# Attention beside a gated recurrence: four engines in written order, one decay copy per level, a third pair of sums on VectorE

## The chip, the cores and the metric

The kernel runs on one core of one Trainium2 chip. The metric is device time in microseconds (us). An engine takes its instructions in the order of its queue; PE is TensorE (PEld its weight loads), DVE is VectorE, ACT is ScalarE, POOL is GpSimd, SP is the queue that issues the DMAs. [...]

## What is computed

One layer of a diffusion backbone over 2048 latent and 256 context tokens, all in fp32: a normalised and modulated input, one projection, then two groups of heads side by side (softmax attention with 8 query and 2 key heads, and a gated linear recurrence with 4 heads that runs in both directions), their joint output projection, and a SwiGLU block. The change is in the two groups of heads:

```python
s = jnp.einsum('bqkgd,bnkd->bkgqn', q, keys).astype(jnp.float32) * scale
p = jax.nn.softmax(s, axis=-1)
return jnp.einsum('bkgqn,bnkd->bqkgd', p.astype(vals.dtype), vals)
...
S_new = jnp.exp(b_last)[..., None] * S + jnp.einsum('bhsk,bhsv->bhkv', kc * jnp.exp(b_last[:, :, None, :] - b), vc)
...
o = rmsnorm(o_f + flip(o_b), gain).reshape(Bn, T, HG_WIDTH)
return (o * jax.nn.silu(g.astype(jnp.float32))).astype(g.dtype)
```

## The kernel before

The program goes through five stages: modulation, projection, attention beside recurrence, output projection, SwiGLU. The change is in the third, the `with` block from line 610 on.

**Attention.** 32 items (16 blocks of 128 queries for each of the 2 key heads), each of 18 steps, one step for each tile of 128 keys. The global step is `x`, `n` the item and `k` the step in it. A step (`Item.scores`, L992) multiplies keys and queries in two matmuls (L1000, L1001: high and low part) into one of three PSUM banks `s`, and ACT takes the exponential into half of a tile `p` (L1004): a pair of steps fills 1024 columns. Beside it a step does one chunk of the next item's maxima (`Item.chunk`, L961): a matmul into one of two banks `mx` (L969, L975) and a reduction on DVE (L971, L977); `Item.maxima` (L983) transposes the result `pn` through a bank of pool `ps_h` and writes it into the next item's queries. Every six steps is an *event* (steps 8, 14 and 20, the last being step 2 of the next item): `Item.products` (L1013) multiplies the last six exponentials by the values (L1020), and sums them over the keys with 32 columns of ones (L1028). The sums take two groups of matmuls for a batch: one over `ps`, the sum of the first two pairs that POOL made (`Item.add`, L1008), one over the third pair `p`. `drain` (L1032) empties the bank, takes the reciprocal of the sums, and `finish` (L1038) scales.

**Recurrence.** A `Unit` (L628) is 512 tokens of a head (unit 0 the 256 of the context). It goes through seven *levels*, in each of which blocks of 1, 2, ... 64 tokens are joined. Two lanes of units run, one level of each per *round*; two rounds fall in an item, at the events of steps 8 and 14. In a round PE makes the scores `pa` from the tiles `Q` and `M` (L684), DVE copies them under a mask into `A` (L694), POOL multiplies `M`, `C` and both halves of `Q` by decays (L703, L706, L715, L717), ACT copies the other halves of `M` and `C` into new tiles (L709, L710), and DVE makes the next level's decays `T` (L721). `prepare` (L649), `diagonal` (L667), `keys` (L726), `forward` (L738), `chain` (L779) and `output` (L786) are steps around it; `output` makes `po` on PE, squares it on ACT, sums it on DVE (L798), takes the root on POOL (L799), and `store` scales it on DVE (L807) and multiplies by the gate on POOL.

**Order.** PE and DVE keep the order in which the code is written (`manual_schedule`, L1080 and L1159; SP too in the first item); the instructions of ACT and POOL are placed by the scheduler from its own estimate of times. At which step a piece of the recurrence is written is set by the table `STEPS` (L1077) and by `Recurrence.plan` (L822). Behind the last item (L1101 on) stand the loads and casts of the output projection's weights (`wos`, `woh` L1121, `wol` L1122) and its first tokens (`mix_token`, L1128).

Of the kernel before, what the change touches and what calls it, by code (L numbers as in the profile page):

```python
# [16 lines left out]
P = 128  # L17
# [51 lines left out]
def block_kernel(ctx: ExitStack, tc: tile.TileContext, a: dict, out: bass.AP, dbg=None):  # L69
# [540 lines left out]
    with ExitStack() as st:  # L610
# [16 lines left out]
        mask = hc.tile([P, 7, P], I32, name="mask")  # L627
        class Unit:  # L628
# [3 lines left out]
            def __init__(self, h, u):  # L632
                self.h, self.u = h, u
                self.n = 256 if u == 0 else 512
                self.nch = self.n // P
                self.t0 = 0 if u == 0 else 256 + (u - 1) * 512
                self.lv = 0
                self.kt = [None, None]

# [9 lines left out]
            def prepare(self):  # L649
                h, u, n, F = self.h, self.u, self.n, self.F  # L650
                M = up.tile([P, 512], F32, tag="M", name=f"M{h}{u}_0", bufs=4)
                C = up.tile([P, 512], F32, tag="C", name=f"C{h}{u}_0", bufs=4)
                pair = "p (j s) -> p j s"
                nc.scalar.activation(M[:, :n].rearrange(pair, s=2), strided(F[:], 0, [[4, n // 2], [3, 2]]),
                                     AF.Identity, scale=-1.0, bias=1.0)
                nc.scalar.activation(C[:, :n].rearrange(pair, s=2), strided(F[:], 1, [[4, n // 2], [1, 2]]),
                                     AF.Identity, scale=-1.0, bias=1.0)
                self.M, self.C, self.T = M, C, F
# [8 lines left out]
            def diagonal(self):  # L667
# [4 lines left out]
                nc.scalar.activation(self.A, pa, AF.Copy)  # L672

# [14 lines left out]
            def level(self, pa=None):  # L688

                h, u, n, lv, M, C, Tt = self.h, self.u, self.n, self.lv, self.M, self.C, self.T  # L690
                hs = 1 << lv
                nb = n // hs
                if u:
                    nc.vector.copy_predicated(  # L694
# [3 lines left out]
                M2 = up.tile([P, 512], F32, tag="M", name=f"M{h}{u}_{lv + 1}", bufs=4)  # L698
                C2 = up.tile([P, 512], F32, tag="C", name=f"C{h}{u}_{lv + 1}", bufs=4)
                g4 = nb // 4  # L700
                odim = [[4 * hs, g4], [3 * hs, 2], [1, hs]]
                if nb >= 4:
                    nc.gpsimd.tensor_tensor(strided(M2[:], 0, odim), strided(M[:], 0, odim),  # L703
                                            strided(Tt[:], 2, [[8, g4], [3, 2], [0, hs]]), op=ALU.mult)
                    idim = [[4 * hs, g4], [hs, 2], [1, hs]]
                    nc.gpsimd.tensor_tensor(strided(C2[:], hs, idim), strided(M[:], hs, idim),  # L706
                                            strided(Tt[:], 1, [[8, g4], [5, 2], [0, hs]]), op=ALU.mult)
                    cdim = [[4 * hs, g4], [1, 2 * hs]]
                    nc.scalar.activation(strided(M2[:], hs, cdim), strided(C[:], hs, cdim), AF.Copy)  # L709
                    nc.scalar.activation(strided(C2[:], 0, odim), strided(C[:], 0, odim), AF.Copy)  # L710
                if u:
                    Q4 = self.Q.rearrange("p d (j s h) -> p d j s h", s=2, h=hs)
                    T3 = Tt[:, :nb, :].rearrange("p (j s) d -> p j s d", s=2)
                    sh = [P, nb // 2, hs]
                    nc.gpsimd.tensor_tensor(Q4[:, 1, :, 1, :], Q4[:, 1, :, 1, :],  # L715
                                            T3[:, :, 0, 0][:, :, None].to_broadcast(sh), op=ALU.mult)
                    nc.gpsimd.tensor_tensor(Q4[:, 0, :, 0, :], Q4[:, 0, :, 0, :],  # L717
                                            T3[:, :, 1, 1][:, :, None].to_broadcast(sh), op=ALU.mult)
                T2 = up.tile([P, nb // 2, 2], F32, tag=f"T{lv}", name=f"T{h}{u}_{lv}",
                             bufs=8 if lv == 6 else 2)  # L720
                nc.vector.tensor_reduce(T2, Tt[:, :nb, :].rearrange("p (j s) d -> p j d s", s=2),  # L721
# [90 lines left out]
        class Recurrence:  # L812
# [40 lines left out]
            def context(self, h):  # L853
# [3 lines left out]
                for _ in range(4):  # L857
                    yield
# [934 lines left out]
```

## Time and profile before

| | |
|---|---|
| median of 3 runs | 3236.01 us (3235.59 to 3236.52) |
| the profiled execution | 3230.49 us, its span 3228.7 us |
| granted PE clock over the span | 0.993 |
| the stretch of attention and recurrence | 727 to 1740 us of the span |
| busy in it: PE, DVE, ACT, POOL | 986, 605, 520, 684 us |
| the 192 groups of sums (L1028) | 2 x 1536 matmul records, 61.9 and 59.5 us busy |
| POOL's 96 additions of pairs (L1011) | 229.9 us, 2395 ns each |
| reductions of the maxima (L971) | 496, 685 ns each |

How to read it: a row of groups gives line, engine, operation, output and inputs, shapes, count, then busy us and the mean ns of one, then the idle time ahead of them with what ended it. A row of the timeline gives start, length, line and operation, and in brackets the idle time ahead of it. A row of waits says who waited for whom, the total, how often, the longest. fp32 matmuls stand twice in the records, once for each of two passes. Matmuls are pipelined, so their busy times overlap.

### The profile page before, as it was taken

What the parts mean: (1) busy time and instruction counts of PE and PEld (TensorE: products, weight loads), DVE (VectorE), ACT (ScalarE), POOL (GpSimd) and SP (SyncE); (2) the same over time, 40 slices, a digit from 0 to 9 for tenths busy, and PEclk for the clock granted to TensorE, in tenths of its full rate; (3) what the DMA queues carried; (4) which work ended last, traced back from release to release, by engine and by line L of the source; (5) the groups of instructions that cost most, each with busy time, mean ns of one, the idle gap of its engine ahead of it and who ended that gap; (6) DMA issues with size and microseconds to landing.
All of it is one profiled execution on the core that took longest, in us unless ns stands there. A gap on an engine that the chain in (4) does not pass through costs nothing. (4 is left out here: it accounts for less than half of the span.)

```text
span 3228.7 us, 55815 instructions
## 1 busy us (share of the span) xinstructions
PE 3145.3 (97%) x21212; PEld 2559.5 (79%) x21212; DVE 1755.1 (54%) x3070; ACT 1326.6 (41%) x2563; POOL 1575.1 (49%) x1403
## 2 busy tenths in 40 slices
PE   8999999999999999999999999999999999999998
PEld 5998987896777777777777887888877778888886
DVE  6344555416666665665653656445458753333566
ACT  4422222215554555554543225333335443333344
POOL 4322222206767767776634226777600168776222
PEclk9999999999999999999999999999999999999999
DMA  7243544324111211211006435555575533332665
GB/s 246 92 137 125 153 145 146 119 93 121 31 36 46 67 34 49 59 37 48 28 21 201 134 115 183 196 179 189 173 291 195 193 111 115 108 104 98 243 195 185
DMA packets 368999, 406.86 MB, mean 126 GB/s; under 512 B 31285, under 2 KB 260889, under 8 KB 368346
## 3 DMA queue, kind: packets, MB, share of 16 engines
q1 hardware_dynamic: 368730, 403.30, 38.9%
q8 instruction: 166, 2.72, 0.4%
q14 instruction: 103, 0.84, 0.1%
HBM read 273.34 MB, written 129.78 MB: 125 GB/s over the span
## 5 line engine op out<-in xcount | busy, mean ns | idle before, releaser
L971 DVE TENSOR_REDUCE mn<-mx 128x1 f32<-128x512 f32 x496 | 333.9, 685 | 209.7 <-PE mx L969 204.6
L1004 ACT ACTIVATE p<-s 128x512 f32<-128x512 f32 x576 | 338.5, 598 | 167.3 <-PE s L1001 147.5
L1011 POOL TENSOR_TENSOR ps<-p,p 128x1024 f32<-128x1024 f32 x96 | 229.9, 2395 | 162.3 <-ACT p L1004 162.3
L1020 PE MATMUL av<-p,VS 128*64 128x256 f32 x2304 | 268.7, 382 | 0.0
L1000 PE MATMUL s<-qa,K 128*128 128x512 f32 x576 | 253.4, 440 | 10.8 <-ACT p L1004 10.8
L1001 PE MATMUL s<-qb,KB 128*128 128x512 f32 x576 | 227.4, 395 | 0.0
L1020 PEld LDWEIGHTS av<-p,VS 128*64 128x64 f32 x2304 | 158.9, 138 | 82.5 <-issue 13.9
L969 PE MATMUL mx<-K,qa 128*128 128x512 f32 x496 | 200.9, 406 | 2.7 <-DVE mn L971 2.4
L1621 DVE TENSOR_TENSOR dl<-dl,x 128x512 fp32r<-128x512 f32 x154 | 113.7, 761 | 70.8 <-ACT x L1614 69.9
L1000 PEld LDWEIGHTS s<-qa,K 128*128 128x128 f32 x576 | 109.0, 189 | 47.9 <-issue 19.8
L1614 ACT ACTIVATE x<-dl 128x512 fp32r<-128x512 f32 x154 | 96.2, 631 | 106.1 <-DMA dl<-s_hid0A 41.1
L1614 ACT ACTIVATE dh<-dl 128x512 fp32r<-128x512 f32 x154 | 89.0, 623 | 93.7 <-PE pd1A L1682 48.3
L345 PE MATMUL f<-hTh,wh 128*128 128x512 f32 (+1 forms) x320 | 120.8, 377 | 6.9 <-ACT ft L374 6.9
L969 PEld LDWEIGHTS mx<-K,qa 128*128 128x128 f32 x496 | 93.4, 188 | 41.4 <-DVE mn L971 17.8
L1621 DVE TENSOR_TENSOR dl<-dl,dh 128x512 fp32r<-128x512 f32 x154 | 102.0, 688 | 43.1 <-ACT dh L1614 42.0
L122 POOL TENSOR_TENSOR rs_xf<-ms_xf,mhalf 128x1 f32<-128x1 f32 x16 | 12.7, 803 | 227.6 <-DVE ms_xf L120 227.6
L345 PE MATMUL f<-hTh,wl 128*128 128x512 f32 (+1 forms) x320 | 118.5, 370 | 0.0
L345 PE MATMUL f<-hTl,wh 128*128 128x512 f32 (+1 forms) x320 | 118.4, 370 | 0.0
L1001 PEld LDWEIGHTS s<-qb,KB 128*128 128x128 f32 x576 | 109.6, 190 | 10.9
L1445 PE MATMUL pA<-x,A22h 128*128 128x512 f32 x352 | 108.9, 391 | 4.5 <-DVE r L1518 4.5
L1445 PE MATMUL pA<-x,A11h 128*128 128x512 f32 x352 | 110.7, 395 | 2.4 <-ACT A11h L1414 2.4
L1445 PE MATMUL pC<-x,A12h 128*128 128x512 f32 x352 | 112.0, 391 | 0.0
(373 smaller groups left out, 9337.0 us busy)
## 6 DMA issues: line engine op xcount, KB each, us to landing
w<-in_w_gu_dram SPq DMA_DIRECT2D x88, 512.0 KB
wm<-in_w_mod_dram SPq DMA_DIRECT2D x24, 1024.0 KB
dl<-s_wT SPq DMA_DIRECT2D x88, 256.0 KB
dl<-s_wB SPq DMA_DIRECT2D x66, 256.0 KB
wq<-in_w_down_dram SPq DMA_DIRECT2D x44, 256.0 KB
s_wT<-wq SPq DMA_DIRECT2D x44, 256.0 KB
dl<-s_hid1S SPq DMA_DIRECT2D x44, 256.0 KB
dl<-s_hid0S SPq DMA_DIRECT2D x44, 256.0 KB
```

The lines of the kernel that those rows point to most:

```text
L122: nc.gpsimd.tensor_tensor(rs, ms, mhalf[:, :width], op=ALU.pow)
L345: nc.tensor.matmul(pm[:, :n], w[wi][:, k, c0:c0 + P], hT[b][hi][:, k, :], start=(k == 0 and i == 0), stop=(k == KT - 1 and i == 2))
L969: nc.tensor.matmul(s, self.qa[:, h * P:(h + 1) * P], K[:, k * 512:(k + 1) * 512], start=True, stop=True)
L971: nc.vector.tensor_reduce(self.mn[:, h, k:k + 1], s, axis=AX.X, op=ALU.min)
L1000: nc.tensor.matmul(s, KS[self.g][:, ks], self.qa, start=True, stop=False)
L1001: nc.tensor.matmul(s, KB[k // BATCH][:, k % BATCH * P:(k % BATCH + 1) * P], self.qb, start=False, stop=True)
L1004: nc.scalar.activation(self.pairs[p][:, o:o + 512], s, AF.Exp, scale=-1.0)
L1011: nc.gpsimd.tensor_tensor(t, self.pairs[p - 1], self.pairs[p], op=ALU.add)
L1020: nc.tensor.matmul(self.av[i * 64:(i + 1) * 64, :256], VS[:, k, self.g * 64:(self.g + 1) * 64], self.pairs[k // 2][:, o:o + 256], start=(k ...
L1445: nc.tensor.matmul(acc, w[wi][:, k, :], x[xi][k], start=(start and k == 0 and i == 0), stop=(stop and k == KH - 1 and i == 2), skip_group_ ...
L1614: nc.scalar.activation(hi, f32v(lo), AF.Copy)
L1621: nc.vector.tensor_tensor(lo, f32v(lo), f32v(hi), op=ALU.subtract)
```

## The change

- **Sums.** A batch is now described by `SUMS = ".PE.PE.PE"`: of each three pairs POOL adds the second to the first (P), and DVE adds the third at the event (E), just ahead of the products. One group of sums is left per batch.
- **Order.** ACT and POOL are written in order too. All pieces of the recurrence stand in lists of global steps; `later` puts an instruction some steps behind.
- **Level.** `C` is changed in place instead of being copied (L710 goes), the two multiplications of `Q` become one instruction of 512 columns, and `T` is made ahead (`extend`): the first at a step of its own, the next ones at the event without a round.
- **Readout.** ACT squares and sums by chunk of 128 (`accum_out`) and scales by chunk, three steps later; DVE's two operations go.
- **Reciprocal.** `drain` copies the sums too, and `invert` takes the reciprocal from SBUF at step 8 instead of step 3; `finish` goes from step 5 to 10.
- **Banks and tiles.** `pn` takes a bank of the `mx` pool. The values are in three tiles of 64 columns, loaded anew for the second key head. Minima chunks start eight instead of six steps ahead.

The core of it (a few of the moved steps' tables and the context's small functions are left out):

```diff
+        LACT, LPOOL, TE = 0, [0, 0, 0], 2
+        KC, STT = 0, 1
...
+        CHAIN, OUT = [121, 110, 102, 98], [129, 117, 108, 100]
+        def later(d, f, *args):
+            if d <= 0:
+                f(*args)
+            else:
+                todo.setdefault(now[0] + d, []).append((f, args))
...
+                def moved():
+                    nc.scalar.activation(strided(M2[:], hs, cdim), strided(C[:], hs, cdim), AF.Copy)
+                def queries():
+                    x = strided(self.Q[:], 0, [[2 * hs, nb // 2], [512 + hs, 2], [1, hs]])
+                    nc.gpsimd.tensor_tensor(x, x, strided(Tt[:], 3, [[4, nb // 2], [-3, 2], [0, hs]]), op=ALU.mult)
+                def crossed():
+                    nc.gpsimd.tensor_tensor(strided(C[:], hs, idim), strided(M[:], hs, idim),
                                             strided(Tt[:], 1, [[8, g4], [5, 2], [0, hs]]), op=ALU.mult)
-                    nc.scalar.activation(strided(C2[:], 0, odim), strided(C[:], 0, odim), AF.Copy)
...
-                nc.scalar.activation(o, po, AF.Square)
-                nc.vector.tensor_reduce(ss, o.rearrange("p (c v) -> p c v", v=P), axis=AX.X, op=ALU.add)
+                for c in range(4):
+                    cs = slice(c * P, (c + 1) * P)
+                    nc.scalar.activation(o[:, cs], po[:, cs], AF.Square, accum_out=ss[:, c:c + 1])
...
-                nc.vector.tensor_tensor(o3, self.po.rearrange("p (c v) -> p c v", v=P),
-                                        self.rs[:, :, None].to_broadcast([P, 4, P]), op=ALU.mult)
+                for c in range(4):
+                    nc.scalar.activation(o3[:, c, :], po[:, c * P:(c + 1) * P], AF.Copy, scale=rs[:, c:c + 1])
...
-                pm = ps_h.tile([P, 512], F32, tag="h", name=f"pn{self.nm}")
+                pm = ps_mx.tile([P, 512], F32, tag="x", name=f"pn{self.nm}")
...
-                if k % BATCH == 3:
-                    self.add(p)
+                if k % 2 and SUMS[p] in "PD":
+                    later(ADD[SUMS[p]], self.add, p)
...
+                (nc.gpsimd if SUMS[p] in "PQ" else nc.vector).tensor_tensor(t, a, self.pairs[p], op=ALU.add)
...
-                for n, t in enumerate((self.sums.pop(b), self.pairs[3 * b + 2])):
+                for p in [p for p in range(k0 // 2, k1 // 2) if SUMS[p] == "."]:
+                    t = self.sums.get(p, self.pairs[p])
...
-                nc.scalar.activation(self.ot, self.av[:, :256], AF.Copy)
-                nc.vector.reciprocal(self.li, self.av[:, 256:384])
+                nc.scalar.activation(self.ot, self.av[:, :384], AF.Copy)
+            def invert(self):
+                self.li = self.ot[:, 256:]
+                nc.vector.reciprocal(self.li, self.li)
...
-        VS = kvp.tile([P, NKT, P], F32, name="VS")
+        VS = [kvp.tile([P, 6, 64], F32, name=f"VS{r}") for r in range(3)]
...
+            for e, t in enumerate(EVENTS):
+                made = rec.round() if e in ROUNDS else iter(())
+                next(made, 0)
+                for p in range(BATCHES[e][0] // 2, BATCHES[e][1] // 2):
+                    if SUMS[p] in "EQ":
+                        items[m].add(p)
+                items[m].products(e)
+                next(made, 0)
+                for ahead, u in rec.decays(x) if e == TE else ():
+                    u.extend(min(ahead, 7))
```

Three places of the order. First PE at the event of step 14 of an item, before (`av` products, `one` the columns of ones; lines of the old kernel):

```order
L969 MATMUL mx_0_2_12217<-K_7830,qa_0_12048 128x512
L684 MATMUL pa_12220<-Q_11942,M_1_12124 64x64 x8
L684 MATMUL pa_12220<-Q_11089,M_5_12135 64x64 x8
L1020 MATMUL av_0_12094<-p_0_3_12051,VS 64x256 x4
L1020 MATMUL av_0_12094<-p_0_4_12069,VS 64x256 x4
L1020 MATMUL av_0_12094<-p_0_5_12154,VS 64x256 x4
L1028 MATMUL av_0_12094<-ps_0_4_12149,one_7838 32x128 x8
L1028 MATMUL av_0_12094<-p_0_5_12154,one_7838 32x128 x8
L1000 MATMUL s_0_15_12287<-qa_0_11180,K_7830 128x512
```

And now, at the same event (lines of the new kernel):

```order
L1040 MATMUL mx_0_4_11851<-K_7830,qa_0_11687 128x512
L709 MATMUL pa_11854<-Q_11586,M_1_11761 64x64 x8
L709 MATMUL pa_11854<-Q_10762,M_5_11763 64x64 x8
L1096 MATMUL av_0_11739<-p_0_3_11690,VS_7836 64x256 x4
L1096 MATMUL av_0_11739<-p_0_4_11710,VS_7836 64x256 x4
L1096 MATMUL av_0_11739<-p_0_5_11784,VS_7836 64x256 x4
L1104 MATMUL av_0_11739<-ps_0_3_11776,one_7840 32x128 x8
L1071 MATMUL s_0_15_11904<-qa_0_10852,K_7830 128x512
```

The group over the third pair `p` is gone; the group that is left reads `ps`, which holds all three pairs. DVE at the same event, before (`mn` reductions of the maxima, `A` the masked copies, `T` the decays, one behind each masked copy):

```order
L971 TENSOR_REDUCE mn_0_12184<-mx_0_2_12217 128x1
L694 COPY_PREDICATED A_11941<-mask,pa_12220 128x512
L721 TENSOR_REDUCE T_1_12274<-T_0_12132 128x256
L694 COPY_PREDICATED A_11088<-mask,pa_12220 128x512
L721 TENSOR_REDUCE T_5_12285<-T_4_12143 128x16
L971 TENSOR_REDUCE mn_0_12184<-mx_0_3_12293 128x1
```

And now (`ps` from `ps` and `p` is the new addition):

```order
L1042 TENSOR_REDUCE mn_0_11789<-mx_0_4_11851 128x1
L1086 TENSOR_TENSOR ps_0_3_11776<-ps_0_3_11776,p_0_5_11784 128x1024
L722 COPY_PREDICATED A_11585<-mask,pa_11854 128x512
L722 COPY_PREDICATED A_10761<-mask,pa_11854 128x512
L1042 TENSOR_REDUCE mn_0_11789<-mx_0_5_11910 128x1
```

The addition of the third pair stands ahead of the masked copies, and the decays have left the event. ACT at the end of the last item, before (`p` exponentials, `woh` casts of the output projection's weights, `ot` the drain, `mh` casts of the first tokens):

```order
L1121 ACTIVATE woh_19774<-wos_19809 128x1024
L1004 ACTIVATE p_1_7_19668<-s_1_15_19701 128x512
L1004 ACTIVATE p_1_8_19707<-s_1_16_19708 128x512
L1121 ACTIVATE woh_19776<-wos_19813 128x1024
L1004 ACTIVATE p_1_8_19707<-s_1_17_19712 128x512
L1121 ACTIVATE woh_19778<-wos_19817 128x1024
L1121 ACTIVATE woh_19780<-wos_19821 128x1024
L1121 ACTIVATE woh_19782<-wos_19825 128x1024
L1034 ACTIVATE ot_1_19744<-av_1_19615 128x256
```

And now:

```order
L1075 ACTIVATE p_1_8_18700<-s_1_16_18701 128x512
L1075 ACTIVATE p_1_8_18700<-s_1_17_18705 128x512
L872 ACTIVATE o_18687<-po_18674,rs_o_18697 128x128 x4
L1110 ACTIVATE ot_1_18736<-av_1_18573 128x384
L1230 ACTIVATE mh_18828<-mix_18821 128x512
L1230 ACTIVATE mh_18828<-mt_18830 128x512
L1230 ACTIVATE mh_18903<-mix_18896 128x512
L1207 ACTIVATE woh_18759<-wos_18788 128x1024
L1207 ACTIVATE woh_18761<-wos_18792 128x1024
```

The casts of the weights and of the first tokens stood between the last exponentials; now they stand behind the drain.

328 lines of the change are left out of this document (184 added, 144 removed).

## Prediction

> **What bounds the kernel now.** I read the page's busy shares first, then the busy time of each engine in the stretch that the change touches (727 to 1740 us, attention beside the recurrence; the instructions outside it keep their order), then what TensorE (PE) and its weight loads (PEld) wait for there, then PE's timeline around one batch of products.
>
> ```profile
> PE 3145.3 (97%) x21212; PEld 2559.5 (79%) x21212; DVE 1755.1 (54%) x3070; ACT 1326.6 (41%) x2563; POOL 1575.1 (49%) x1403
> 727.00:1740.00 1013.00, 985.96 (x10091) 734.91 (x10090) 605.31 (x1078) 520.20 (x1049) 683.62 (x718) 0.99 0.19 55
> ```
>
> The second row reads: length, then busy PE, PEld, DVE, ACT, POOL. PE is busy 986 of 1013 us; no other engine passes 68%. So PE's own work sets the stretch, and what is left besides is the sum of its stalls:
>
> ```profile
> PE s L1000 <- ACT p L1004: 10.8, 8, 2.4
> PE pn L986 <- DVE o L807: 8.9, 4, 2.3
> PE mx L969 <- DVE mn L971: 2.4, 5, 0.6
> PE pn L986 <- DVE Sb L777: 2.0, 3, 0.7
> PE po L792 <- DVE o L807: 1.7, 1, 1.7
> PEld mx L969 <- DVE mn L971: 17.8, 42, 1.0
> PEld s L1000 <- ACT p L1004: 16.4, 17, 2.8
> ```
>
> Columns: us in total, times, longest. Three causes: the exponentials' results (10.8 + 16.4 = 27 us, the rows partly lying behind other PE work), the minima's reductions on VectorE (20 us, the same way), and a PSUM bank of the recurrence that VectorE empties late (8.9 + 2.0 + 1.7 = 12.6 us).
>
> PE busy overlaps itself, so I price PE work by the distance of starts. One event of the sixth step, two rounds' scores (pa), then a batch of products (av) and sums (one):
>
> ```profile
> 1106.43 0.39 PE L1000 MATMUL s<-qa,K 128*128 128x512 f32 x1
> ...
> 1106.89 0.39 PE L969 MATMUL mx<-K,qa 128*128 128x512 f32 x1
> 1107.21 1.15 PE L684 MATMUL pa<-Q,M 128*64 128x64 f32 x32
> 1108.19 2.76 PE L1020 MATMUL av<-p,VS 128*64 128x256 f32 x24
> 1110.88 0.64 PE L1028 MATMUL av<-ps,one 128*32 128x128 f32 x16
> 1111.34 0.62 PE L1028 MATMUL av<-p,one 128*32 128x128 f32 x16
> 1111.89 0.50 PE L1000 MATMUL s<-qa,K 128*128 128x512 f32 x1
> ```
>
> A plain step is three matmuls (the row left out is the second); the third starts 0.46 us after the first, so they stand 0.23 us apart and a step takes 0.69 us. pa takes 0.98, av 2.69, one group of sums 0.46 us (1110.88 to 1111.34).
>
> **The change part by part.**
>
> *One group of sums less.* The third pair is added to the first two on VectorE, so each batch ends with one group instead of two.
>
> ```profile
> L1028 PE MATMUL av<-ps,one 128*32 128x128 f32 x1536 | 61.9, 279 | 0.0
> L1028 PE MATMUL av<-p,one 128*32 128x128 f32 x1536 | 59.5, 273 | 0.0
> ```
>
> 1536 records are 96 groups of 16 (two passes of 8), one per batch and row. The busy column would promise 59.5 us; by starts it is 96 x 0.46 = 44 us, and I take 44 because the next matmul cannot start earlier than that. It lies wholly on the path: **-44 us**, bounds 42 (0.44 where the hand-over is shorter) and 59.5.
>
> *What VectorE pays.* 96 adds of 128x1024. VectorE's nearest rows:
>
> ```profile
> L971 DVE TENSOR_REDUCE mn<-mx 128x1 f32<-128x512 f32 x496 | 333.9, 685 | 209.7 <-PE mx L969 204.6
> L694 DVE COPY_PREDICATED A<-mask,pa 128x512 f32<-128x512 int32 x112 | 82.2, 739 | 22.4 <-PE pa L684 20.9 <-ACT M L709 1.4 <-DMA q<-s_hq 0.2
> L721 DVE TENSOR_REDUCE T<-F 128x512 f32<-128x1024 f32 x16 | 19.3, 1204 | 0.0
> L807 DVE TENSOR_TENSOR o<-po,rs_o 128x512 f32<-128x512 f32 x16 | 11.0, 687 | 11.9 <-POOL rs_o L800 11.9
> L1036 DVE RECIPROCAL li<-av 128x128 f32<-128x128 f32 x32 | 30.6, 958 | 105.1 <-ACT ot L1034 105.1
> L798 DVE TENSOR_REDUCE sso<-o 128x4 f32<-128x512 f32 x16 | 11.0, 686 | 43.6 <-ACT o L796 43.6
> L1011 POOL TENSOR_TENSOR ps<-p,p 128x1024 f32<-128x1024 f32 x96 | 229.9, 2395 | 162.3 <-ACT p L1004 162.3
> 1727.53 1.23 DVE L1122 TENSOR_TENSOR wol<-wos,woh 128x1024 fp32r<-128x1024 f32 x1 [2.81 <-ACT woh L1121]
> 1728.12 2.88 POOL L1011 TENSOR_TENSOR ps<-p,p 128x1024 f32<-128x1024 f32 x1 [1.54 <-ACT p L1004]
> ```
>
> A two-operand pass over 1024 columns of SBUF takes 1.23 us: 96 x 1.23 = 118 us more, less 22 us for the two readout operations of 11.0 us that leave VectorE. 605 + 96 = about 701 busy us of some 965: the engine has room on average. Locally it has less. In a plain step it needs 0.69 us for one reduction, and PE's step is 0.69 us. The room is in the events: there mn + add + two masked copies are 0.69 + 1.23 + 1.48 = 3.4 us against PE's 0.98 + 2.69 + 0.46 = 4.1. The sums need the add after 0.69 + 1.23 = 1.92 us; PE reaches them after 3.67 us with pa and 2.69 us in the event without pa: a slack of 1.75 and 0.77 us. At step 8 the moved reciprocal (0.96 us) stands ahead of the add and cuts 1.75 to 0.79.
>
> Behind the add VectorE's queue holds the masked copies and the next reductions, for which PE's two mx banks wait. And the add is the first operation of this stretch that reads two SBUF operands on VectorE. The trace has that elsewhere:
>
> ```profile
> 1765.21 1.72 DVE L1251 TENSOR_TENSOR x<-x,xn 128x512 f32<-128x512 f32 x1
> 1770.65 0.69 DVE L1251 TENSOR_TENSOR x<-x,xn 128x512 f32<-128x512 f32 x1
> 1765.10 1.29 POOL L1145 TENSOR_TENSOR ml<-mix,mh 128x512 fp32r<-128x512 f32 x1 [7.33 <-ACT mh L1144]
> ```
>
> The same add takes 0.69 us alone and 1.72 us when a GpSimd (POOL) operation began 0.11 us earlier: 1.03 us held. Started first, as at 1727.53, it takes its 1.23 us, and POOL's add takes 2.88 instead of the mean of 2.40 us. The add cannot meet POOL's own 1024-wide sum of its batch, since it reads that sum; it can meet the 512-wide operations of a round or a preparation. Held 1.03 us, it is 1.03 - 0.77 = 0.26 us late in the 32 events without pa: **+8 us**. Bounds: 0 (POOL idle at that moment, which is likely where queries wait for pa) and 96 x 1.03 = 99 us (no slack left anywhere).
>
> [...]
>
> The first decay product (L721, 1.2 us, 16 times) leaves its place behind a masked copy. Four of them now stand at step 14 ahead of the add, where 0.69 + 1.2 + 1.23 = 3.1 us are still under 3.67. Twelve stand in plain steps (5 and 12), where nothing covers them but the second mx bank (0.69 us): 12 x 0.5 = **+6 us**, bounds 0 and 14.
>
> *The readout and the bank.* At a readout PE stops so:
>
> ```profile
> 1017.47 0.27 PE L986 MATMUL pn<-identr,neg 128*4 128x128 f32 x1 [2.24 <-DVE o L807]
> 1018.50 1.98 PE L684 MATMUL pa<-Q,M 128*64 128x64 f32 x32
> 1020.27 3.40 PE L1020 MATMUL av<-p,VS 128*64 128x256 f32 x24
> 1023.60 0.64 PE L1028 MATMUL av<-ps,one 128*32 128x128 f32 x16
> ```
>
> The maxima's transpose waits for the bank that L807 empties, and afterwards pa takes 1.77 instead of 0.98 us and av 3.33 instead of 2.69: 1.4 us more, three times, 4 us. The change gives that transpose a bank of the mx pool and lets ScalarE empty po. So 12.6 + 4 = **-17 us**; if another matmul inherits the wait, 0.
>
> *ScalarE (ACT) and POOL in written order.*
>
> ```profile
> L1004 ACT ACTIVATE p<-s 128x512 f32<-128x512 f32 x576 | 338.5, 598 | 167.3 <-PE s L1001 147.5
> ACT M L654 <- DMA F<-s_f: 22.4, 5, 5.7
> ```
>
> ACT loses one copy per level (140 in all) and gains eight short operations for each of 16 readouts in place of one; at 520 of 1013 us this costs nothing, its idle time hides it, and if an exponential (0.60 us) is held by them it counts with the next term. That term is whether an exponential stands behind something that is not ready: 27 us of PE's waits now, and one cause is seen in the second row, preparations that wait for their load. In the new order the context's preparation stands seven steps behind its load, and the drain of av behind an exponential that needs the same PE time. I take a third of the 27 away: **-10 us**, bounds -27 and +27. POOL does the same arithmetic in fewer instructions; its 330 idle us hide what that shifts, and without this cover the slower rival below begins. The values tile in three loads of 64 columns is asked for eight steps before the first batch (8 x 0.69 = 5.5 us hide it; late, it costs a few us once), and the two minima chunks that come earlier are as many as before: nothing.
>
> *The end of the stretch.* Before, the scheduler put the casts of w_out between the last exponentials:
>
> ```profile
> 1700.00:1740.00 40.00, 39.86 (x350) 28.63 (x349) 13.88 (x16) 20.65 (x33) 27.02 (x17) 1.00 0.70 220
> 1718.09 2.95 ACT L1121 ACTIVATE woh<-wos 128x1024 fp32r<-128x1024 f32 x3
> 1736.55 1.06 ACT L1121 ACTIVATE woh<-wos 128x1024 fp32r<-128x1024 f32 x1 [2.88 <-DMA wos<-in_w_out_dram]
> ```
>
> PE had no gap. Now ACT and POOL come to these casts only after the drain. The chain of loads and casts took 1737.6 - 1718.1 = 19.5 us; PE has the first token's 48 matmuls to do meanwhile, 48 x 0.23 = 11 us. The rest, **+8 us**, is new idle time; bounds 2 and 19.
>
> **The sum.** -44 + 8 + 6 - 17 - 10 + 8 = -49 us. The profiled execution took 3230.5 us (span 3228.7, 1.8 around it): 3181.5. The median of the runs is 5.5 us above that execution, so 3187 us.
>
> **The rivals.**
>
> *Everything clears.* The written order also removes the other waits for exponentials and the adds never meet POOL: -44 - 17 - 27 + 2 = -86, 3150 us. For it: the reductions wait 204.6 us for PE, so VectorE is ahead most of the time. Against it: the plain steps, where PE, VectorE (0.69) and ACT (about 0.6) are within a tenth of each other.
>
> *The waits only change places.* The bank stall goes to another matmul, ACT in order holds exponentials for 27 us more, the end costs 12: -44 + 8 + 6 + 27 + 12 = +9 at worst, and with half of the 27 about -4: 3232 us, no change. For it: an order by hand cannot step around a late DMA, and ACT waited 22 us for such loads.
>
> *Slower: VectorE is the late engine at the sums.* If POOL runs behind, its own sum ends near the event, the add then starts late, and the reductions behind it hold PE as well. The other terms are -44 - 17 - 10 + 6 + 8 = -57, so it decides from 57 / 96 = 0.59 us of lateness per batch on. At a full 1.03 us the sum is -57 + 99 = +42: 3278 us. For it: POOL is 68% busy and its sum now stands behind a whole round in written order. Against it: the sum is asked for five plain steps and a product batch ahead of its use.
>
> **How the numbers follow.** Forecast 0.62, everything clears 0.18, change of places 0.10, slower by the add 0.10. Range: from 3163 us (two thirds of the way from the forecast's -49 to the -86 of the clearing case) to 3222 us (the forecast with the bank stall kept and no gain on ACT, -22, is 3214, and 8 us over); the 3232 and 3278 us are left out. About 0.2%, 6.5 us, is what a measurement of this kernel can tell from no change. Faster by more are the first two cases and 0.04 of the third, 0.84; within it 0.05 of the third and 0.01 of the last, 0.06; slower by more the rest, 0.10.
>
> **What would show it.** The changed profile should have one group of sums at 1536 records and none on p; the stretch about 45 us shorter with PE still over 95% busy; no wait of pn on the readout; the VectorE add with a mean between 1.23 and 1.7 us. PE waiting for the add at the sums for over 40 us in total would make the slower rival right; a gap of over 15 us after the last product batch would make the end's term wrong; waits on exponentials above 27 us would make ACT's term wrong.

## The result, and the profile after

| | before | changed |
|---|---|---|
| median of the runs | 3235.80 us (4 runs, 3233.57 to 3236.52) | 3198.78 us (4 runs, 3195.74 to 3204.73) |
| profiled execution, span | 3230.49, 3228.7 us | 3204.73, 3202.6 us |
| ratio of times | | 0.9889, 95% interval 0.9872 to 0.9906 |

The changed kernel is 37 us faster; the forecast was 49 us, 3187 us, with a range that holds the result. The changed kernel's profiled execution is the slowest of its four, 6 us above their median, so differences of a few us are taken from medians and from several kernels' traces, not from this one trace.

The page of the changed kernel, then the stretch of attention (the row's columns are those of the row shown of before: length, then busy PE, PEld, DVE, ACT, POOL, the granted clock, DMA share, GB/s), and the 40 us behind it:

```profile
PE 3110.2 (97%) x19676; PEld 2528.0 (79%) x19676; DVE 1878.1 (59%) x3134; ACT 1290.0 (40%) x2599; POOL 1617.5 (51%) x1291
```

```profile
727.00:1680.00 953.00, 928.88 (x8502) 690.11 (x8501) 717.99 (x1135) 473.21 (x1074) 709.81 (x600) 1.00 0.19 52
1680.00:1720.00 40.00, 30.88 (x105) 21.26 (x106) 15.31 (x19) 13.42 (x21) 15.80 (x9) 0.79 0.83 259
```

The last sums end at 1679.1 instead of 1734.3 us, 55 us earlier. Not all of that is gained: some 6 us of it are matmuls of the output projection (`mt` and `y`) that stood ahead of the last sums before and stand behind them now. And behind the last sums PE is busy for 31 of 40 us at a clock of 0.79, where before it had no gap behind them:

```profile
1735.00:1775.00 40.00, 40.00 (x186) 33.22 (x185) 19.31 (x32) 9.99 (x22) 7.25 (x7) 1.00 0.64 202
```

That gives back a good part. In the stretch, PE and its weight loads now wait for other things than before (us in total, times, longest):

```profile
PE av L1104 <- DVE ps L1086: 8.1, 7, 3.2
PE mx L1040 <- DVE mn L1042: 6.7, 12, 1.0
```

```profile
PEld mx L1040 <- DVE mn L1042: 17.1, 21, 1.4
PEld av L1104 <- DVE ps L1086: 16.5, 20, 3.7
```

The two tall rows of before, scores waiting for exponentials (10.8 us) and pn for the readout (8.9 us), are gone. In their place stand the sums waiting for VectorE's add, and the matmuls mx waiting for their reductions, 6.7 us instead of 2.4. The groups of the sums and of the add (count, busy us, mean ns, idle ahead and by whom):

```profile
L1104 PE MATMUL av<-ps,one 128*32 128x128 f32 x1536 | 62.3, 280 | 8.2 <-DVE ps L1086 8.1
```

```profile
L1086 DVE TENSOR_TENSOR ps<-ps,p 128x1024 f32<-128x1024 f32 x96 | 142.4, 1484 | 10.5 <-ACT p L1075 9.7 <-POOL ps L1086 0.8
L722 DVE COPY_PREDICATED A<-mask,pa 128x512 f32<-128x512 int32 x112 | 75.8, 727 | 0.0
```

One group is left, and none on p; the add's mean is 1.48 us, inside the 1.23 to 1.7 us that were forecast.

To see what the stalls sum to, I list every distance between two of PE's starts that is over 0.45 us, from the first mx to the last sums or the first matmul of the output projection, whichever comes first, less the 0.23 us at which the matmuls stand, by the matmul that was late (us, worked out from the trace's records):

| late matmul, its cause | before | two groups of sums (below) | changed | carries in events (below) |
|---|---|---|---|---|
| s, exponentials | 12.7 | 0.3 | 0.4 | 0.5 |
| pn, readout's bank, then the reductions | 11.7 | 2.6 | 2.6 | 6.6 |
| mx, reductions | 4.4 | 12.5 | 12.8 | 3.3 |
| sums, VectorE's add | 0.0 | 0.0 | 9.1 | 0.6 |
| pa, pd, po, pk and others | 4.0 | 8.2 | 6.8 | 7.1 |
| all | 32.8 | 23.6 | 31.7 | 18.1 |

Columns one and three carry the result: the stalls that the prediction wanted gone went (21 us), and almost as many came in. Of the 55 us by which the last sums end earlier, 42 are the group of sums (a batch's sums take 1.01 us before and 0.57 us now, the median from their first start to the start behind them), 6 the matmuls that moved and 1 the stalls. Some 3 us more are the clock: by the trace's record of it, it was halved for 13.7 us of the stretch before and for 6.8 us now, and about half of such time is lost: in the 6.8 us of now, from 807.58 on, the matmuls of a plain step stand 0.43 us apart instead of 0.23. The last 3 us are not placed.

### The profile page after: what moved, and what is told of

It is laid out like the page before. It is cut to its first block, busy times and chain, and to the rows that moved or that the text cites. A ratio compares the mean times of both kernels' runs of the same rounds, so it can differ in the third digit from the quotient of the medians.

```text
span 3202.6 us, 52755 instructions
## 1 busy us (share of the span) xinstructions
PE 3110.2 (97%) x19676; PEld 2528.0 (79%) x19676; DVE 1878.1 (59%) x3134; ACT 1290.0 (40%) x2599; POOL 1617.5 (51%) x1291
## 5 line engine op out<-in xcount | busy, mean ns | idle before, releaser
L743 POOL TENSOR_TENSOR Q<-Q,T 128x512 f32<-128x512 f32 x96 | 141.2, 1488 | 18.3 <-PE pa L709 17.9
L1086 DVE TENSOR_TENSOR ps<-ps,p 128x1024 f32<-128x1024 f32 x96 | 142.4, 1484 | 10.5 <-ACT p L1075 9.7
L1071 PEld LDWEIGHTS s<-qa,K 128*128 128x128 f32 x576 | 109.1, 189 | 32.5 <-issue 19.5
L122 POOL TENSOR_TENSOR rs_xf<-ms_xf,mhalf 128x1 f32<-128x1 f32 x16 | 12.7, 800 | 228.7 <-DVE ms_xf L120 228.7
```

What stands on the lines that cost most here:

```text
L1071: nc.tensor.matmul(s, KS[self.g][:, ks], self.qa, start=True, stop=False)
L1086: (nc.gpsimd if SUMS[p] in "PQ" else nc.vector).tensor_tensor(t, a, self.pairs[p], op=ALU.add)
```

## The experiments

All times are medians; each kernel's ratio is to the kernel before, run on the same chip. Where a kernel is compared with the changed one, that is 3198.78 us and 0.9889; differences by medians, as given here, and by ratios lie within 5 us of each other.

**Two groups of sums again.** One string tells which pairs GpSimd (P) and VectorE at the event (E) add:

```diff
-        SUMS, ADD = ".PE.PE.PE", {'P': 0, 'D': 1}
+        SUMS, ADD = ".P..P..P.", {'P': 0, 'D': 1}
```

> The changed kernel with the third pair left out of the addition: two groups of sums per batch again, no add on VectorE; everything else stays. Theory (the group is on the path at 0.46 us, the add waits little): the group costs 96 x 0.46 = 44 us, and the waits that go with the add are some 8 us of matmuls and what the two mx banks lost by it (4 us); so 32 to 40 us slower than the changed kernel, 3231 to 3239 us. Rival 1 (VectorE pays much of it back, spread over the reductions): 10 to 20 us slower than the changed kernel, and PE's waits on mn fall by more than 10 us. Rival 2 (a group is worth its busy time, 59.5 us in 96): over 50 us slower.

Measured: 3230.51 us, ratio 0.9993 (0.9981 to 1.0004); 32 us slower than the changed kernel. Both groups are there again:

```profile
L1104 PE MATMUL av<-ps,one 128*32 128x128 f32 x1536 | 61.8, 279 | 0.0
L1104 PE MATMUL av<-p,one 128*32 128x128 f32 x1536 | 59.5, 273 | 0.0
```

The theory holds to within a us of its lower edge, 3231 us. PE's wait on mn hardly moves (6.7 us in the changed kernel), so rival 1 falls, and rival 2 with it:

```profile
PE mx L1040 <- DVE mn L1042: 5.8, 11, 1.0
```

A finding that was not asked for: without the add, all the rest of this large change together is worth nothing that can be measured. Its stalls are 9 us fewer (column two of the table), and the end of the stretch, which is the next experiment, costs more than that.

**The last readout earlier.** In the kernel before the last output stands at step 3 of the last row; in the changed kernel at step 15. The experiment puts it back to 3:

```diff
-        CHAIN_LAST, OUT_LAST = [119, 112, 108, 99], [123, 114, 112, 103]
+        CHAIN_LAST, OUT_LAST = [109, 105, 102, 99], [111, 107, 104, 101]
```

> The changed kernel with the last head's chain and output steps some 12 steps earlier (last output at step 3 of the last row, as in the kernel before, where it is at step 15 now). Theory (what was mis-sized at the end of the stretch is the place of the last readout: its buffers hold the memory that w_out is loaded into, so the loads, not the written order of ScalarE, make the casts late): 12 to 24 us faster than the changed kernel, 3175 to 3187 us, the casts stand between the last exponentials and PE has no gap over 2 us after the last product batch. Rival (the written order of ScalarE and GpSimd keeps the casts behind the drain): within 4 us of the changed kernel, and the casts still begin after the last drain.

**ScalarE and GpSimd free in the last row.** The rival to it: written order ends for these two engines nine steps before the end.

```diff
-            if x == NKT:
+            if x in (NKT, NKT * NIT - 9):
                 border.close()
-                border.enter_context(tc.manual_schedule(engines={mybir.EngineType.PE, mybir.EngineType.DVE, mybir.EngineType.Activation, mybir.EngineType.Pool}))
+                border.enter_context(tc.manual_schedule(engines={mybir.EngineType.PE, mybir.EngineType.DVE} | ({mybir.EngineType.Activation, mybir.EngineType.Pool} if x == NKT else set())))
```

> The changed kernel with ScalarE and GpSimd left to the scheduler in the second half of the last row. Theory (the last readout's buffers hold the memory): no difference, within 4 us of the changed kernel, casts after the drain. Rival (the written order keeps the casts behind the drain, as the prediction had it): 10 to 20 us faster.

Measured: the early readout 3185.21 us, 0.9854 (0.9835 to 0.9873), 14 us faster than the changed kernel; the free order 3200.07 us, 0.9906 (0.9889 to 0.9922), no difference. The casts of w_out on ScalarE, with the last drain (L1110) among them, first in the changed kernel, then with the early readout, then with the free order:

```profile
1679.50 0.51 ACT L1110 ACTIVATE ot<-av 128x384 f32<-128x384 f32 x1
1683.88 2.94 ACT L1207 ACTIVATE woh<-wos 128x1024 fp32r<-128x1024 f32 x3
1694.09 1.06 ACT L1207 ACTIVATE woh<-wos 128x1024 fp32r<-128x1024 f32 x1 [6.79 <-DMA wos<-in_w_out_dram]
...
1706.95 1.06 ACT L1207 ACTIVATE woh<-wos 128x1024 fp32r<-128x1024 f32 x1 [3.86 <-DMA wos<-in_w_out_dram]
```

```profile
1669.83 2.94 ACT L1207 ACTIVATE woh<-wos 128x1024 fp32r<-128x1024 f32 x3
1672.67 1.07 ACT L1075 ACTIVATE p<-s 128x512 f32<-128x512 f32 x2
...
1690.01 1.06 ACT L1207 ACTIVATE woh<-wos 128x1024 fp32r<-128x1024 f32 x1 [2.52 <-DMA wos<-in_w_out_dram]
1690.97 0.47 ACT L1110 ACTIVATE ot<-av 128x384 f32<-128x384 f32 x1
```

```profile
1670.80 0.51 ACT L1110 ACTIVATE ot<-av 128x384 f32<-128x384 f32 x1
1674.55 3.10 ACT L1207 ACTIVATE woh<-wos 128x1024 fp32r<-128x1024 f32 x3
```

The theory of the early readout holds by its time (14 us, 11 by ratios) and by the place of the casts, and the rival of the written order falls. With the early readout the casts stand among the exponentials and are over before the drain, although the written order is untouched; with the free order and the late readout they still begin behind the drain. And PE has no gap over 0.7 us any more behind the last product batch, 38.7 busy us of 40 at full clock:

```profile
1680.00:1720.00 40.00, 38.74 (x188) 29.71 (x185) 19.59 (x28) 12.37 (x23) 10.31 (x8) 1.00 0.74 231
```

The loads move with the readout. SyncE's queue issues the first three of w_out here, in the changed kernel and with the early readout:

```profile
1669.58 1.52 SPq L1206 DMA_DIRECT2D wos<-in_w_out_dram  x3
```

```profile
1656.77 1.49 SPq L1206 DMA_DIRECT2D wos<-in_w_out_dram  x3
```

But late loads are not what makes the first casts late, as the theory had it. In the changed kernel the loads are issued 2.4 us before the last readout's first matmul (1671.98), and by the updates of their semaphores in the trace they have landed at 1674.11, 1677.02 and 1678.28, over 5 us before the first cast at 1683.88. What ends just ahead of that cast is the store of the last readout's result, here first in the changed kernel, then with the early readout:

```profile
1681.00 0.36 SPq L1185 DMA_DIRECT2D s_hg<-o  x1
```

```profile
1665.37 0.36 SPq L1261 DMA_DIRECT2D s_hg<-o  x1
```

The stores have landed at 1683.43 and 1669.46 us, and the first casts start 0.45 and 0.37 us later. Between the two, ScalarE's queue holds a wait for the semaphore of that store; in ten of the eleven kernels that were made here from the one before, such a wait among the first three casts ends 0.02 us after the landing. In the changed kernel the first cast also stands behind the drain and three casts of tokens, so the store alone is not shown to hold it; with the free order the first two casts start before the store has landed, and the third waits for it. The later casts do wait for their loads (6.79 and 3.86 us in the rows above), and those are issued only from 1688.76 on, behind the first casts. That the casts write where the readout's tiles lay is read from the code (the recurrence's pools are closed ahead of w_out's). The runs show that the place of the last chain and readout sets the time of the casts, and in the traces the store of its result is the last thing that they wait for.

**ScalarE and GpSimd free throughout.** The two engines are taken out of both `manual_schedule` calls.

> The changed kernel with ScalarE and GpSimd left to the scheduler throughout, as in the kernel before; all else stays. Theory (it is the written order that took PE's waits on exponentials away, 27 us before and under 1 us now): 15 to 27 us slower than the changed kernel, and the waits of the scores and their weight loads on p are above 15 us again. Rival (they went because ScalarE has one copy less per level and because the readout no longer stands between exponentials as one long operation): within 5 us of the changed kernel and waits on p under 5 us.

Measured: 3206.03 us, 0.9922 (0.9909 to 0.9936): 7 us slower than the changed kernel, 6 than the one with the free last row, between theory and rival. Its waits on exponentials:

```profile
PE s L1071 <- ACT p L1075: 3.6, 3, 1.2
```

```profile
PEld s L1071 <- ACT p L1075: 6.5, 8, 1.6
```

10 of the 27 us come back with the scheduler's order, 17 don't; by the distances of starts it is 4.5 us at s, against 12.7 before and 0.4 in the changed kernel. The written order is worth some 6 us; something else took the other waits.

**The bank back.** `maxima` takes pn from `ps_h` again, as before.

> The changed kernel with the maxima's transpose (pn) in the recurrence's bank again, as before. Theory (the bank was worth what the prediction put on it, 12.6 us of stalls and 4 us of slow clock behind them): 10 to 17 us slower than the changed kernel, and pn or the matmul ahead of it waits for the readout again by over 8 us. Rival (ScalarE empties the readout in four pieces and sooner, so the bank is free by then whichever bank it is): within 4 us of the changed kernel, and pn waits under 3 us.

**ScalarE's copy twice.** `moved` issues its copy a second time.

> The changed kernel with ScalarE's one copy per level issued twice (the same data to the same place), so that ScalarE does as many copies as before, in the written order. Theory (about 17 of the 27 us of waits on exponentials went with the copies, the rest with the order): waits of the scores on p come back to 8 us or more, and the kernel is 5 to 12 us slower than the changed one. Rival (ScalarE has room for them wherever they stand): waits on p stay under 3 us, within 4 us of the changed kernel.

Measured: bank back 3200.78 us, 0.9900 (0.9885 to 0.9915); copy twice 3202.55 us, 0.9904 (0.9887 to 0.9920). Neither differs measurably from the changed kernel. With the bank back, pn waits again, for half of what it did before:

```profile
PE pn L1057 <- ACT o L872: 4.5, 3, 1.5
...
PE pn L1057 <- ACT kb L640: 1.4, 3, 0.5
```

The times speak for the bank's rival, the waits lie between the two. The copies' theory falls: with twice the copies PE still waits for no exponential. What remains as the cause of the cleared waits are the new places of the readout's steps and its shorter operations. No run moves these alone, so this stays argued, not shown.

**The add in a plain step.** On the kernel with the early last readout: `SUMS = ".PD.PD.PD"`, VectorE adds one step after the pair's second exponential.

> The kernel with the early last readout, and VectorE's add one step after its pair's second exponential, in a plain step, instead of at the event. Theory (only the events have room: in a plain step VectorE has 0.69 us of reduction and 1.23 us of add against PE's 0.69 us, and the second mx bank covers 0.69 us of it): 0.5 us lost per batch, 96 x 0.5 = 48 us, less some 5 us of waits at the sums: 35 to 50 us slower than the kernel with the early last readout, 3220 to 3235 us, with PE's waits on mn up by over 30 us. Rival (VectorE is ahead by more than one step, since its reductions wait 175 us for PE): within 6 us of that kernel, and waits of the sums on the add gone.

Measured: 3194.87 us, 0.9886 (0.9871 to 0.9901): 10 us slower than with the add at the event, between theory and rival. No sum waits for the add any more, and the reductions cost more:

```profile
PE mx L1040 <- DVE mn L1042: 11.6, 15, 1.2
```

```profile
PEld mx L1040 <- DVE mn L1042: 25.0, 27, 1.6
```

The event is the right place, but my price for a plain step was four times too high. That the sums' waits that go and what VectorE catches up over the following steps make up for most of it is likely, but no run separates the two.

**Without the scaling of the queries.** On the kernel with the early last readout, `level` leaves out GpSimd's scaling of Q.

> The kernel with the early last readout, and without the scaling of the queries by the decays at every level (GpSimd's Q<-Q,T and Q<-Q,F are left out, so the queries stay unscaled). Theory (VectorE's add is long where GpSimd's Q is under way): the add's mean falls from 1.43 us at the first event of a row to under 1.3 us, and the kernel is 3 to 10 us faster than with them, 3175 to 3182 us, because the waits of the sums on the add go, and those of pa on Q. Rival (the add's length and lateness come from VectorE's own queue): the add's mean stays above 1.4 us, within 3 us.

Measured: 3184.04 us, 0.9853 (0.9838 to 0.9867), no difference from the kernel with the scaling (3185.21). The add, there and here:

```profile
L1086 DVE TENSOR_TENSOR ps<-ps,p 128x1024 f32<-128x1024 f32 x96 | 137.8, 1435 | 6.4 <-POOL ps L1086 3.4 <-ACT p L1075 2.9
```

```profile
L1086 DVE TENSOR_TENSOR ps<-ps,p 128x1024 f32<-128x1024 f32 x96 | 130.0, 1354 | 7.5 <-POOL ps L1086 4.6 <-ACT p L1075 2.9
```

GpSimd's scaling does lengthen the add, by 81 ns in the mean (1435 against 1354), and the sums' waits on it fall from 4.8 to 1.4 us, but that does not reach the time: most of the lengthening lies in the slack. The theory has the mechanism and not the price (at the first event the mean falls to 1.34, not below 1.3 us).

**Carries in events.** By the table above the largest new stall is mx, and it is there with two groups as well, so the add isn't its cause. In the changed kernel VectorE's queue shows what is, with PE's late matmul beside it:

```profile
960.92 0.69 DVE L1042 TENSOR_REDUCE mn<-mx 128x1 f32<-128x512 f32 x1 [0.89 <-PE mx L1040]
961.53 1.49 DVE L803 SCALAR_TENSOR_TENSOR S<-S,T,psf 128x128 f32<-128x128 f32 x4
962.94 1.96 DVE L1042 TENSOR_REDUCE mn<-mx 128x1 f32<-128x512 f32 x3
```

```profile
962.35 0.39 PE L1072 MATMUL s<-qb,KB 128*128 128x512 f32 x1
963.67 0.50 PE L1040 MATMUL mx<-K,qa 128*128 128x512 f32 x1 [0.93 <-DVE mn L1042]
```

Four carries of the recurrence, 1.49 us, stand between two reductions in a plain step; the next mx comes 1.32 instead of 0.23 us after its neighbour. On the kernel with the early last readout I let the carries run at the end of the next event, and moved the blocks that feed them:

```diff
-        PREP, DIAG, EXT, FWD, READ = [1, 27, 64, 91], [4, 31, 67, 94], [5, 32, 66, 95], [12, 41, 75, 93], 96
-        CHAIN, OUT = [121, 110, 102, 98], [129, 117, 108, 100]
+        PREP, DIAG, EXT, FWD, READ = [1, 27, 64, 91], [4, 31, 67, 94], [5, 32, 66, 95], [14, 44, 80, 92], 96
+        CHAIN, OUT = [122, 116, 104, 98], [129, 117, 108, 100]
...
-                later(STT, self.carry, ps, S)
+                (hold.append((self.carry, (ps, S))) if self.u else later(STT, self.carry, ps, S))
...
                 items[m].products(e)
+                while hold: (lambda f, a: f(*a))(*hold.pop(0))
```

The chain's carry is held in the same way, except for the last head.

> The kernel with the early last readout, and VectorE's carries of the recurrence (four operations of 0.35 us after each block of psf or psb) moved from plain steps into events, behind the add; the matmuls that feed them move to the same events (the last head's own chain stays). Theory (the new waits of the matmuls mx, 4.4 us in the kernel before and 12.8 us in the changed one by the gaps of PE's starts, come from carries of 1.4 us that now stand in plain steps): those waits fall under 6 us and the kernel is 5 to 10 us faster than with the early readout alone, 3175 to 3180 us. Rival (the events have no room left behind the add, or the recurrence's two banks are held there): PE waits at pa or at the sums instead, within 4 us of that kernel or slower.

**The readout's scaling on VectorE.** The same base, with one multiplication of 0.69 us on VectorE in `store` in place of four operations on ScalarE.

> The kernel with the early last readout, and the readout's scaling on VectorE again (one operation of 0.69 us for four on ScalarE), in a plain step. Theory (VectorE's plain steps have no room, so what stands there costs PE what the second mx bank doesn't cover): 16 x 0.45 = 7 us slower at most, 3187 to 3193 us, and the waits of mx on mn up by 3 to 7 us. Rival (one such operation is within the cover): within 3 us.

Measured: carries in events 3171.87 us, 0.9820 (0.9805 to 0.9836), 13 us faster than the early readout alone; the scaling on VectorE 3190.14 us, 0.9870 (0.9855 to 0.9886), 5 us slower than it, with intervals that overlap. The first theory holds and gains more than its 5 to 10 us; the second holds by its time. In the kernel with the carries in events mx hardly waits any more (3.3 us by starts, where it was 12.9 with the early readout), and the sums hardly wait for the add (1.38 us in the mean instead of 1.44):

```profile
L1040 PE MATMUL mx<-K,qa 128*128 128x512 f32 x489 | 195.2, 399 | 0.4 <-ACT mr L1059 0.2
L1104 PE MATMUL av<-ps,one 128*32 128x128 f32 x1536 | 61.9, 279 | 0.5 <-DVE ps L1086 0.5
```

All stalls fall from 30.6 (early readout) to 18.1 us, though pn takes over 4 us of what mx loses, and the time falls by 13 us, 11 by ratios. This kernel is the fastest here: 22 (by ratios) to 27 us (by medians) below the changed one, and 60 us below the kernel before, 3232.08 us beside it. With the scaling on VectorE, PE's wait for mn goes from 5.8 to

```profile
PE mx L1040 <- DVE mn L1042: 9.8, 11, 1.5
```

But by the distances of starts mx stands where it did (13.1 us against 12.9), and the sums for more (10.4 against 5.7 up to the last sums), with two adds of over 3 us in this one trace. So what the 5 us are is not shown.

## Why the prediction was right, and where its steps were not

The sign, the main term and the slack behind it were right; two terms were mis-sized, one cause was wrong, and one step of the change was not seen.

| term | forecast | measured |
|---|---|---|
| one group of sums less, and the add held | -44 + 8 = -36 | -32 (two groups) |
| end of the stretch | +8 | +14 (early last readout) |
| order on ScalarE and GpSimd | -10 | about -6 (free throughout) |
| bank of pn | -17 | -2, within the error (bank back) |
| first decays in plain steps | +6 | at most +3, from the trace alone |
| carries moved into plain steps | not seen | +13, what moving them out of there gives |
| sum of all | -49 | -37 |

The rows were undone one at a time and on different bases, and they don't add up: the third to sixth come to between +5 and +8 us, where the whole leaves -19 for them (-37 + 32 - 14). The stall table says where the difference lies. From before to changed, the waits for exponentials fall by 12.3 us and those of pn by 9.1, those of mx and the others grow by 8.4 and 2.8, and the clock gives some 3. With -42 + 9 for the sums and +14 for the end that is about -32, which is 5 us short of -37; one trace can differ from a median by as much. So 21 us of waits did go, but undoing the order brought back only 4 of them by starts, and the old bank 4. For some 13 us no run shows which part of the change took them.

That the time fell so close to the forecast is therefore in part luck. The order and the bank were given 27 us and the runs credit them with 8; the carries cost 13 us that no term had, the end 6 us more than its term; and the 13 us without a shown cause make up for much of that.

*The sums.* By PE's starts the sums of a batch fall from 1.01 to 0.57 us, 42 us in 96, not 44. The waits for the add take 9.1 us in the changed kernel's trace, and 3.2 to 6.8 us in those of the five kernels above that keep the add at its event and the carries where they are (early readout, free order in the last row and throughout, bank back, copy twice). That this is near the +8 is luck, since the way there was another: I put all waits into the 32 events without pa. There the add took 1.27 us in the mean, hardly held at all, and came late once. In the trace the add ends 0.8, 1.4 and 0.9 us (medians) ahead of the end of the products in the first, second and third batch of a row, so there is slack in all of them. It lacks at seven single adds, and two very long ones (below) make 5.9 of the 9.1 us. The slower rival is out: it needed 0.59 us of lateness per batch, and 9.1 / 96 is 0.09.

In the trace the add is longer where GpSimd works: the 22 adds that met no GpSimd operation took 1.23 us at most, the 74 others 1.56 us in the mean. The measured price is a tenth of the upper bound of 99 us, a hold of 1.03 us at every add with no slack, since most adds were held for less than 1.03 us and had the slack above.

*The end of the stretch failed as a step.* The prediction said: "Now ACT and POOL come to these casts only after the drain." They do, but not for the written order's sake: with the two engines left to the scheduler in the last row nothing changes, and with the last chain and readout 12 steps earlier the casts are back among the exponentials. The last readout was 12 steps later than before, and its store ends just ahead of the first cast. I had the tables `CHAIN_LAST` and `OUT_LAST` before me and costed them nowhere. The size was off too: the chain from the first cast to the last takes from 1683.9 to 1708.0, 24 us instead of the 19.5 taken over from before, PE is idle for 9 of the 40 us behind the stretch, and for 17 us of them the clock was halved (1681.39 and 1705.28, at the end of this document). The gap of over 15 us that I had named as refuting the term did not come, since the idle time lies in pieces of at most 2 us between slow matmuls.

*The readout and the bank: right sum, wrong cause.* The stall went, but not through the bank: with the old bank only half of pn's waits come back and no measurable time. Why the exponentials' waits went is open in the same way: the order accounts for 10 of 27 us, the copies for none.

*What was missed.* "If another matmul inherits the wait, 0" was written for the bank and was true of the stretch: mx inherited 8 us. The carries' new places were in the change's tables, and VectorE's plain steps are exactly where the prediction said there is no room. That was applied to the decays (+6, where the late starts around the twelve come to 3 us at most in the trace) and not to the carries (1.4 us in one piece, with mx 1.1 us late at seven places).

The rival that waits only change places (3232 us) described the stretch better than the forecast: of 33 us of stalls 32 remain. It missed the result because it priced ScalarE's order at +14 to +27 us, where the order gains. One reading was loose: VectorE's add is not the first operation of 727 to 1740 us with two SBUF operands there, since the row of `wol` at 1727.53 lies in that stretch too; the sum does not hang on it.

## What to carry to other kernels

When an engine with a short step takes over new work, list every operation that the same change moves on that engine, and ask of each group in one piece whether it is longer than what the consumer's buffers cover; a group of four carries, 1.4 us in a plain step, made the next matmul 1.1 us late, while a 1.2 us add with 0.8 us of slack or more mostly cost nothing. Where the next stage begins in memory that this stage used, the last user of that memory (here, by the code, the store of the last readout) is part of the path into it, and a table that moves it deserves a term of its own. Look in the trace for the wait that ends last: here the loads looked late and had long landed. And count the stalls as a whole before and after, not only those that should go: here 21 us went and 20 came.

## What the runs showed of the hardware

An add on VectorE lasted as long as a whole run of GpSimd's operations, twice in 96. In the changed kernel one add took 6.23 us (those that met no GpSimd operation took 1.23 at most) and PE's sums stood for it; at the same moment GpSimd began the first of six more operations:

```profile
801.94 6.23 DVE L1086 TENSOR_TENSOR ps<-ps,p 128x1024 f32<-128x1024 f32 x1
```

```profile
801.95 1.45 POOL L738 TENSOR_TENSOR M<-M,T 128x256 f32<-128x256 f32 x2
803.36 2.34 POOL L743 TENSOR_TENSOR Q<-Q,T 128x512 f32<-128x512 f32 x2
805.66 1.43 POOL L746 TENSOR_TENSOR C<-M,T 128x256 f32<-128x256 f32 x2
```

The six end at 807.09, the add 1.08 us later: by its length it was held for the whole run, not for one. A second one of 4.47 us is alike, 1.09 us past the end of a run:

```profile
1500.63 4.47 DVE L1086 TENSOR_TENSOR ps<-ps,p 128x1024 f32<-128x1024 f32 x1
```

The other 72 adds that met GpSimd took 2.35 us at most, so what makes an add last a whole run is open. The two cost PE about 6 us (gaps of 3.61 and 2.76 us at the sums), as much as this execution lies above its median; the profiled execution with the free last row has none and is the lowest of its kernel. That they make the spread of the runs is a guess.

The clock also fell beside short pauses. In the 40 us behind the stretch PE's longest idle time is 1.98 us, and the clock was halved twice, by the trace's record of it from 1681.39 for 10.2 us and from 1705.28 for 6.8 us. The rows below cut these at other places (granted clock 0.64, 0.53, 1.00, 0.52):

```profile
1680.00:1685.00 5.00, 3.03 (x11) 1.93 (x11) 2.07 (x3) 2.66 (x6) 3.14 (x3) 0.64 0.50 136
1685.00:1692.00 7.00, 5.63 (x14) 3.99 (x15) 3.38 (x2) 2.30 (x3) 5.96 (x3) 0.53 0.92 279
1692.00:1705.00 13.00, 8.25 (x35) 5.31 (x33) 2.88 (x2) 4.23 (x4) 4.21 (x2) 1.00 1.01 353
1705.00:1712.00 7.00, 5.98 (x12) 3.41 (x13) 2.61 (x4) 2.00 (x3) 0.76 (x2) 0.52 0.27 89
```

The piece from 1692 on was less busy than its neighbours (8.25 of 13 us) and ran at full clock, so the busy share of a piece alone does not tell its clock. Pauses of under 2 us went along with half clock here: the one of 1.98 us stands just ahead of the first slow piece, and the second began during a pause of 1.69 us; with one of 1.63 us at 1693.57 the clock stayed full. What sets the clock, the trace does not show.
